# Taking every fourth weight remainder from an accumulating DMA in a two-layer trunk (GLA and spatial gating)

## The chip, the cores and the metric

The kernel runs on one core of a Trainium2 chip. The metric is the time of one execution in microseconds of device time; lower is better. The kernel before takes 775.23 us (median of two runs, 775.1 and 775.36).

## What is computed

One sequence of 256 tokens with 2048 channels goes through two layers. Layer 0 is a gated linear attention in chunks of 64 tokens, layer 1 a spatial gating with a 128 x 128 position matrix per channel group. Both begin with an RMS norm and a wide input projection, and end with an output projection and a second RMS norm. All arrays are float32.

```python
def reference(x, norm_pre, norm_post, gla_w_in, ..., sgu_w_out):
    for i in range(DEPTH):                       # DEPTH = 2
        h = rmsnorm(x, norm_pre[i])
        if i % N_MIXERS == 0:
            y = gla_mixer(h, ...)                # proj = h @ w_in; ... ; return o @ w_out
        else:
            y = sgu_mixer(h, ...)                # proj = h @ w_in; ... ; return (u * vs * silu(g)) @ w_out
        x = x + rmsnorm(y, norm_post[i])
    return x
```

Nearly all the work is in the four products with the weight matrices: 2048 x 6160 and 2048 x 2048 in layer 0, 2048 x 6144 and 2048 x 2048 in layer 1.

## The kernel before

**Tiles and steps.** The columns of the four weight matrices are cut into 33 groups, almost all of 512 columns (the three groups for the keys have 352, 344 and 344). A group's 16 K tiles of 128 rows are taken two at a time (KC = 2), so a group has 8 steps, and the program 264, numbered from 0 across all groups. Both tiles of 128 tokens (t = 0 and t = 1) use a step's weights, one after the other.

**Two parts of each number.** A product is made from float32r parts. A weight is split into `whi`, its rounded value, and `wlo`, the remainder; activations are split in the same way. Three matmuls per K tile and tile of tokens stand for one exact product (lines 178 to 180): xh·whi, xl·whi, xh·wlo. A step is thus 2 K tiles x 2 tiles of tokens x 3 = 12 matmuls.

**How a step's weights come.** `load` has SP issue a DMA of 128 x 1024 floats (512 KB) into a buffer `raw`, of which there are four (RAWS). `split` has ACT cast `raw` to `whi` (line 110), and DVE subtract `whi` from `raw` into `wlo` (line 111). At 8 steps near the start, around the layer boundary and at the end POOL subtracts in DVE's place (START, POOL). Of `whi` and `wlo` there are six buffers each (SPLITS). So the cast of step j cannot begin before the matmuls of step j - 6 are through, and the load of step j cannot begin before the split of step j - 4 has read its `raw`.

**The order.** Engines take their instructions in the order in which the program writes them. `run` writes a step's matmuls, then one stage of whatever follows earlier groups (evacuations, norms, transposes, attention), then `fetch` for the steps up to four ahead (AHEAD). Hence on ACT the cast of step 8g + 11 stands behind the evacuation of tile 0 of group g, which itself waits for the last matmul of step 8g + 7 with that tile. Around the boundary between the layers (step 136) the tiles of tokens take turns of five steps (LAG).

**Other work on POOL.** POOL carries few instructions: powers for the norms (line 224), two products per tile of tokens in the groups for u (line 703), products for the boundary (lines 605, 640), some memsets, and the 8 subtractions. It issues no DMA.

Of the kernel before, what the change touches and what calls it, by code (L numbers as in the profile page):

```python
# [9 lines left out]
F32R = mybir.dt.float32r  # L10
BF16 = mybir.dt.bfloat16
AF = mybir.ActivationFunctionType
ALU = mybir.AluOpType
PSUM = bass.MemoryType.PSUM

P = 128
# [6 lines left out]
KC = 2  # L23
LAG = 5
# [5 lines left out]
SLOTS = 24  # L30
RAWS = 4
SPLITS = 6


@with_exitstack
def trunk(
# [18 lines left out]
    nc = tc.nc  # L55
# [9 lines left out]
    of = out[0]  # L65
# [6 lines left out]
    wraw = ctx.enter_context(tc.tile_pool(name="wraw", bufs=RAWS))  # L72
    wsp = ctx.enter_context(tc.tile_pool(name="wsp", bufs=SPLITS))
    gains = ctx.enter_context(tc.tile_pool(name="gains", bufs=3))
# [12 lines left out]
    def w512(name, dtype=F32):  # L87
        return work.tile([P, 512], dtype, name=name, tag="w512")

# [1 line left out]
    def load(parts, c, fine):  # L91
        w = sum(n for _, _, n in parts)
        raw = wraw.tile([P, KC, w], F32, name="raw", tag="raw")
        at = 0
        for src, c0, n in parts:
            rows = src[c * KC * P : (c + 1) * KC * P, c0 : c0 + n].rearrange("(a p) n -> p a n", p=P)
            for ks in pieces(fine):
                nc.sync.dma_start(raw[:, ks, at : at + n], rows[:, ks, :])
            at += n
        return raw  # L100

    def pieces(fine):
        return [slice(k, k + 1) for k in range(KC)] if fine else [slice(0, KC)]

    def split(raw, eng, fine):
        shape = [P, KC, raw.shape[2]]
        hi = wsp.tile(shape, F32R, name="whi", tag="whi")
        lo = wsp.tile(shape, F32R, name="wlo", tag="wlo")
        for ks in pieces(fine):
            nc.scalar.copy(hi[:, ks], raw[:, ks])  # L110
            eng.tensor_tensor(lo[:, ks], raw[:, ks], hi[:, ks].bitcast(F32), op=ALU.subtract)  # L111
        return hi, lo

    NS = KT // KC

    class Stream:
        """Projections, column group by column group, in steps of KC K tiles; both tiles of
        tokens use a step's weights. What follows a group's products is a generator, whose
        stages come one by one between the parts that follow; a stage may ask for more parts
        before the next. Around a boundary (a group whose operand is the end of all groups  # L120
        before it) the tiles of tokens take turns of LAG steps, so that each one's products
        cover what the other waits for."""

        def __init__(self, groups, boundaries, mid):
            self.mid = mid
# [19 lines left out]
        def fetch(self, i):  # L145
            if i < len(self.steps) and i not in self.split:
                self.load(i)
                eng = nc.gpsimd if i in self.pool_lo else nc.vector
                self.split[i] = split(self.raw[i], eng, i == 0)

        def start(self, gen):
            if gen is not None:
# [35 lines left out]
        def run(self):  # L188
            freed, at = 0, 0
            for i, t in self.order:  # L190
# [4 lines left out]
                at = max(at, i)  # L195
                for j in range(at + 1, min(at + (AHEAD if at >= NS else 2), freed + SPLITS - 1) + 1):
                    self.fetch(j)
# [1 line left out]
                self.advance()  # L199

    def split_T(dst, t, c, tp):
        """Four transposed blocks, from PSUM into the two parts of a product's operand."""
        ah, al = dst
        sl = slice(t * P, (t + 1) * P)
        nc.scalar.copy(ah[c][:, :, sl], tp)  # L205
        nc.vector.tensor_tensor(al[c][:, :, sl], tp, ah[c][:, :, sl].bitcast(F32), op=ALU.subtract)  # L206
# [7 lines left out]
    def new_T(name):  # L214
        return (
            [slot(S4, F32R, f"{name}h{c}") for c in range(4)],
            [slot(S4, F32R, f"{name}l{c}") for c in range(4)],
        )
# [18 lines left out]
        return rstd(s1, D, name)  # L237

    def bcast(vecs, cs):
        """Column groups of vectors, on every partition."""  # L240
        g = gains.tile([P, 2, 512], F32, name="gb", tag="gb")
        for i, (v, c) in enumerate(zip(vecs, cs)):
            nc.sync.dma_start(
                g[:, i, :], v[c * 512 : (c + 1) * 512].unsqueeze(0).to_broadcast([P, 512])
            )
        return g

# [1 line left out]
    xs = [const.tile([P, D], F32, name=f"x{t}", tag=f"x{t}") for t in range(NT)]  # L249
    vec = const.tile([16, P], F32, name="vec")  # L250
    nc.scalar.dma_start(vec, norm_pre[0].rearrange("(a p) -> a p", p=P))
# [6 lines left out]
    make_identity(nc, ident)  # L258
    mhalf = const.tile([P, 1], F32, name="mhalf")
    nc.gpsimd.memset(mhalf, -0.5)  # L260
    # suffix sums within a chunk: U[t', t] = 1/tau where t' > t and both lie in one chunk;
    # the last two columns give the chunks' sums
    U = const.tile([P, P + 2], F32, name="U")
    nc.gpsimd.memset(U, 0.0)
    for c in range(2):
        r = slice(c * C, (c + 1) * C)
# [7 lines left out]
    gpre0 = const.tile([P, KT], F32, name="gpre0")  # L274
    bsp = const.tile([P, GROUPS], F32, name="bsp")

# [1 line left out]
    hT = new_T("hT")  # L278

    def make_hT(t, c):  # L280
        tp = transpose4(xs[t][:, c * 512 : (c + 1) * 512])
        tmp = w512("ttmp").rearrange("p (a b) -> p a b", b=P)
        gain = gpre0[:, c * 4 : c * 4 + 4].unsqueeze(2).to_broadcast([P, 4, P])
        nc.vector.tensor_tensor(tmp, tp, gain, op=ALU.mult)
        split_T(hT, t, c, tmp)
# [3 lines left out]
    groups = []  # L289

    q, k, la, ek, kd, k2, qT = ([None] * 2 for _ in range(7))
# [14 lines left out]
    for i in range(2):  # L306
        groups.append(dict(parts=[(W, q0 + i * 512, 512)], lhs=lambda: hT, done=q_done(i)))

    # the gate's weights and bias, each part at its own partitions, against the parts of the
    # low-rank activations: one pass gives all four products  # L310
    wg = [None]

    def pre_gate():
# [179 lines left out]
    for i, (c0, n) in enumerate(kcols):  # L493
        parts = [(W, k0 + c0, n)] + ([(W, l0, RANK)] if i == 0 else [])
        groups.append(dict(parts=parts, lhs=lambda: hT, done=k_done(i)))

    on = [None] * HEADS
# [58 lines left out]
    for h in range(HEADS):  # L556
        groups.append(dict(parts=[(W, g0 + h * DV, DV)], lhs=lambda: hT, done=g_done(h)))

# [1 line left out]
    def out_groups(key, w_out, gain, name, end, extra=None):  # L560
        yg = [None] * 4
        ss = [small(f"{name}ss{t}", 4) for t in range(NT)]
# [30 lines left out]

    r1 = [None] * NT

    # the second layer's operand is x1 * gain = x * gain + rstd * (y * post gain * gain)
    yp, xp = [None] * 4, [None] * 4

    def extra0(t, c, ps):
# [45 lines left out]
    groups += gs  # L645
    layer1 = len(groups)

# [1 line left out]
    W2 = sgu_w_in[0]  # L649
    vg = [None] * 4  # L650
    bst = [small(f"bst{t}", 4 * 6).rearrange("p (c s) -> p c s", s=6) for t in range(NT)]
# [42 lines left out]
    def u_done(c):  # L694
        def f(t, ps):
            if t == 0:
                u[c] = slot([P, NT, 512], F32, f"u{c}")
            nc.scalar.activation(u[c][:, t, :], ps, AF.Gelu_apprx_tanh, scale=r1[t])
            a = vg[c][:, t, :]
            mu, rv = st["ln", t]  # L700
            nc.vector.tensor_scalar(a, a, mu, rv, op0=ALU.subtract, op1=ALU.mult)  # L701
            for i, op in enumerate((ALU.mult, ALU.add)):
                nc.gpsimd.tensor_tensor(a, a, st["lng"][:, i, :], op=op)  # L703
        return f

    for c in range(4):
        groups.append(
            dict(
                parts=[(W2, c * 512, 512)], lhs=lambda: st["h2"], done=u_done(c),
# [48 lines left out]

    groups += out_groups("tT", sgu_w_out[0], norm_post[1], "y1", end1)

# [1 line left out]
    mid = {(0, 0): lambda: make_hT(1, 0), (1, 0): lambda: make_hT(0, 1)}  # L762
    for c in range(1, 4):
        mid[2 * c - 1, 1] = lambda c=c: make_hT(1, c)
# [2 lines left out]
    s = Stream(groups, [layer1, len(groups)], mid)  # L767
# [50 lines left out]
```

## Time and profile before

| | before |
|---|---|
| time, median of two runs | 775.23 us |
| span of the profiled execution | 772.0 us |
| PE busy | 755.7 us (98%) |
| DVE busy | 452.9 us (59%) |
| ACT busy | 353.7 us (46%) |
| POOL busy | 87.6 us (11%) |
| DMA engines, share of 16 engines' span in SP's queue | 59.5% |
| read from device memory | 143.55 MB |

The profiled execution's span is 3.2 us below the median time of the runs. PE's busy time counts pipelined matmuls, so it says that PE had matmuls to run nearly always, and not how fast it ran them.

### The profile page before, as it was taken

To read this page: it belongs to the slowest core of one execution; us is meant where nothing else is said; L and a number is where in the kernel's file an instruction comes from. 1 tells how busy PE (TensorE), PEld (TensorE's weight loads), DVE (VectorE), ACT (ScalarE), POOL (GpSimd) and SP (SyncE) were. 2 spreads that over 40 slices of the span, in tenths; PEclk is the share of its full clock that TensorE was granted. 3 is DMA by queue.
4 is the path that set the end of the run, shared out by engine and by line. 5 is a ranking of instruction groups with operands and counts; after the bars stand their busy time and mean duration, and the time that the engine had idled before them with its cause. 6 is when DMAs were issued, how large, how long until landed. Compare 5 with 4: busy or idle time off the path is not lost.

```text
span 772.0 us, 9465 instructions
## 1 busy us (share of the span) xinstructions
PE 755.7 (98%) x3560; PEld 633.4 (82%) x3560; DVE 452.9 (59%) x521; ACT 353.7 (46%) x473; POOL 87.6 (11%) x81
## 2 busy tenths in 40 slices
PE   8999999999999999999989999999999999999995
PEld 6889998888888888888867888888888888888884
DVE  4666764645465545766588564555556565565443
ACT  4654753534354434444446454444335445344430
POOL 3210010000000001403041000132232000000000
PEclk9999999999999999999999999999999999999998
DMA  9576583465755567664724855666766455656633
GB/s 302 162 209 186 159 259 110 136 218 165 216 166 168 169 196 232 215 219 167 264 88 137 272 190 192 196 208 215 227 217 203 152 166 169 195 182 234 203 104 110
DMA packets 81318, 146.28 MB, mean 189 GB/s; under 512 B 7196, under 2 KB 14900, under 8 KB 81272
## 3 DMA queue, kind: packets, MB, share of 16 engines
q1 hardware_dynamic: 81240, 145.66, 59.5%
q8 instruction: 28, 0.46, 0.2%
q14 instruction: 18, 0.15, 0.1%
q10 hardware_dynamic: 32, 0.01, 0.0%
HBM read 143.55 MB, written 2.10 MB: 189 GB/s over the span
## 4 chain that ended last, share of the span: by engine, by line
PE 94%; DVE 2%; issue 1%; DMA 1%; ACT 0%; SPq 0%; POOLq 0%; POOL 0%; DVEq 0%; ACTq 0%
PE acc L180 30%; PE acc L178 30%; PE acc L179 30%; PE tp L211 2%; PE op L519 1%; DVE hp L614 1%; DMA raw<-in_gla_w_in_dram 1%; PE sc L440 1%; PE sp L371 0%; PE sc L433 0%; DVE h2l L206 0%; DVE wlo L111 0%; DVE x L752 0%; DVE x L590 0%; PE sc L446 0%
## 5 line engine op out<-in xcount | busy, mean ns | idle before, releaser
L111 DVE TENSOR_TENSOR wlo<-raw,whi 128x1024 fp32r<-128x1024 f32 (+2 forms) x257 | 316.6, 1254 | 119.6 <-ACT whi L110 119.2
L110 ACT CAST whi<-raw 128x1024 fp32r<-128x1024 f32 (+3 forms) x265 | 264.7, 1021 | 141.7 <-PE acc L179 57.5
L178 PE MATMUL acc<-whi,hTh 128*128 128x512 f32 (+2 forms) x416 | 158.7, 382 | 1.4 <-ACT hTh L205 1.4
L179 PE MATMUL acc<-whi,hTl 128*128 128x512 f32 (+2 forms) x416 | 155.9, 375 | 0.2 <-DVE hTl L206 0.2
L180 PE MATMUL acc<-wlo,hTh 128*128 128x512 f32 (+2 forms) x416 | 156.0, 375 | 0.0
L178 PE MATMUL acc<-whi,h2h 128*128 128x512 f32 x384 | 151.5, 394 | 0.0
L179 PE MATMUL acc<-whi,h2l 128*128 128x512 f32 x384 | 150.0, 391 | 0.0
L180 PE MATMUL acc<-wlo,h2h 128*128 128x512 f32 x384 | 149.8, 390 | 0.0
L178 PEld LDWEIGHTS acc<-whi,hTh 128*128 128x128 f32 x416 | 78.5, 189 | 13.3 <-ACT hTh L205 1.7
L180 PEld LDWEIGHTS acc<-wlo,hTh 128*128 128x128 f32 x416 | 78.4, 189 | 12.9
L179 PEld LDWEIGHTS acc<-whi,hTl 128*128 128x128 f32 x416 | 78.6, 189 | 12.7 <-DVE hTl L206 0.6
L180 PEld LDWEIGHTS acc<-wlo,h2h 128*128 128x128 f32 x384 | 72.4, 188 | 15.3
L178 PEld LDWEIGHTS acc<-whi,h2h 128*128 128x128 f32 x384 | 72.4, 189 | 14.4
L179 PEld LDWEIGHTS acc<-whi,h2l 128*128 128x128 f32 x384 | 72.4, 189 | 14.3
L178 PE MATMUL acc<-whi,ogTh 128*128 128x512 f32 x128 | 50.2, 392 | 0.0
L178 PE MATMUL acc<-whi,tTh 128*128 128x512 f32 x128 | 50.0, 391 | 0.0
L179 PE MATMUL acc<-whi,tTl 128*128 128x512 f32 x128 | 49.8, 389 | 0.0
L180 PE MATMUL acc<-wlo,ogTh 128*128 128x512 f32 x128 | 49.8, 389 | 0.0
L180 PE MATMUL acc<-wlo,tTh 128*128 128x512 f32 x128 | 49.8, 389 | 0.0
L179 PE MATMUL acc<-whi,ogTl 128*128 128x512 f32 x128 | 49.8, 389 | 0.0
L703 POOL TENSOR_TENSOR vg<-vg,gb 128x512 f32<-128x512 f32 x16 | 27.8, 1735 | 61.4 <-DVE vg L701 41.1
L229 ACT ACTIVATE sq<-acc 128x512 bf16<-128x512 f32 x16 | 9.5, 596 | 50.3 <-PE acc L180 50.3
(155 smaller groups left out, 586.9 us busy)
## 6 DMA issues: line engine op xcount, KB each, us to landing
raw<-in_sgu_w_in_dram SPq DMA_DIRECT2D x96, 512.0 KB, 4.8
raw<-in_gla_w_in_dram SPq DMA_DIRECT2D x79, 512.0 KB, 4.6
raw<-in_gla_w_out_dram SPq DMA_DIRECT2D x32, 512.0 KB, 5.7
raw<-in_sgu_w_out_dram SPq DMA_DIRECT2D x32, 512.0 KB, 4.8
raw<-in_gla_w_in_dram SPq DMA_DIRECT2D x16, 344.0 KB, 3.7
raw<-in_gla_w_in_dram SPq DMA_DIRECT2D x8, 336.0 KB, 3.6
x<-in_x_dram SPq DMA_DIRECT2D x8, 256.0 KB, 7.4
gb<-in_norm_post_dram SPq DMA_DIRECT2D x8, 256.0 KB, 6.2
```

Of the source, the lines that this page charges most:

```text
L110: nc.scalar.copy(hi[:, ks], raw[:, ks])
L111: eng.tensor_tensor(lo[:, ks], raw[:, ks], hi[:, ks].bitcast(F32), op=ALU.subtract)
L178: nc.tensor.matmul(pt, xh, wh[:, k, :], start=kt == 0, stop=False)
L179: nc.tensor.matmul(pt, xl, wh[:, k, :], start=False, stop=False)
L180: nc.tensor.matmul(pt, xh, wl[:, k, :], start=False, stop=kt == KT - 1)
L211: nc.tensor.transpose(tp[:, k, :], src[:, k * P : (k + 1) * P], ident)
L229: nc.scalar.activation(sq[:, : src.shape[1]], src, AF.Square, accum_out=dst)
L440: nc.tensor.matmul(sc[:, o + C : o + P], k2[c][:, i, o : o + P], qT[c][:, i, o + C : o + P], start=jl == 0, stop=jl == JH - 1,)
L519: nc.tensor.matmul(op, a, b, start=i == 0, stop=i == len(ops) - 1)
L614: nc.vector.scalar_tensor_tensor(hp[c], yp[c][:, t, :], r, xp[c][:, t, :], op0=ALU.mult, op1=ALU.add)
L703: nc.gpsimd.tensor_tensor(a, a, st["lng"][:, i, :], op=op)
```

## The change

In the steps whose number is 3 modulo 4, from step 8 on and in groups with one weight part, `split` gives way to a new function `added`. There ACT writes `wlo` as minus the rounded `raw` (an activation with scale -1), then casts `raw` to `whi` as before. Then POOL issues two DMAs, one for each K tile, that read the same weights from device memory again and add them onto `wlo`. DVE (or POOL) subtracts nothing in these steps. The group of keys with two parts is left as it was, so 62 of the 264 steps change, with 124 DMAs: 58 steps of 512 columns and 4 of 344. The other lines of the diff drop comments; the changed kernel's line numbers are 19 higher behind the new code.

```diff
+ADDED = 4
...
+    def added(raw, src):
+
+        shape = [P, KC, raw.shape[2]]
+        hi = wsp.tile(shape, F32R, name="whi", tag="whi")
+        lo = wsp.tile(shape, F32R, name="wlo", tag="wlo")
+        nc.scalar.activation(lo, raw, AF.Copy, scale=-1.0)
+        nc.scalar.copy(hi, raw)
+        (w, c0, n), c = src
+        for k in range(KC):
+            r = (c * KC + k) * P
+            nc.gpsimd.dma_start(lo[:, k, :], w[r : r + P, c0 : c0 + n], accum_op=ALU.add)
+        return hi, lo
...
         def fetch(self, i):
             if i < len(self.steps) and i not in self.split:
                 self.load(i)
-                eng = nc.gpsimd if i in self.pool_lo else nc.vector
-                self.split[i] = split(self.raw[i], eng, i == 0)
+                g, c = self.steps[i]
+                parts = self.groups[g]["parts"]
+                if len(parts) == 1 and i % ADDED == ADDED - 1 and i >= NS:
+                    self.split[i] = added(self.raw[i], (parts[0], c))
+                else:
+                    eng = nc.gpsimd if i in self.pool_lo else nc.vector
+                    self.split[i] = split(self.raw[i], eng, i == 0)
```

On ACT, the place shown is the end of a group for u (`u` is the evacuation of a tile of tokens, `whi` the cast of a step's weights). Before:

```order
L698 ACTIVATE u_4267<-acc,r_3530 128x512
L110 CAST whi<-raw 128x1024
L698 ACTIVATE u_4267<-acc,r_3597 128x512
L110 CAST whi<-raw 128x1024 x7
L698 ACTIVATE u_4425<-acc,r_3530 128x512
```

The same place on ACT in the changed kernel:

```order
L717 ACTIVATE u_4347<-acc,r_3592 128x512
L111 ACTIVATE wlo<-raw 128x1024
L112 CAST whi<-raw 128x1024
L717 ACTIVATE u_4347<-acc,r_3661 128x512
L124 CAST whi<-raw 128x1024 x3
L111 ACTIVATE wlo<-raw 128x1024
L112 CAST whi<-raw 128x1024
L124 CAST whi<-raw 128x1024 x3
L717 ACTIVATE u_4509<-acc,r_3592 128x512
```

Of the eight steps between two evacuations of tile 0, two have one more ACT instruction, which stands ahead of their cast; one of the two steps is the one right behind the evacuation of tile 0.

On POOL, the place is the boundary between the layers (`y0r` is the norm's power of a tile of tokens, `xp` a product for the next layer's operand). Before:

```order
L224 TENSOR_TENSOR y0r_3305<-y0r_ms,mhalf 128x1
L605 TENSOR_TENSOR xp_3308<-x_87,gb 128x512
L111 TENSOR_TENSOR wlo<-raw,whi 128x1024 x2
L224 TENSOR_TENSOR y0r_3403<-y0r_ms,mhalf 128x1
L605 TENSOR_TENSOR xp_3308<-x_88,gb 128x512
L111 TENSOR_TENSOR wlo<-raw,whi 128x1024
L224 TENSOR_TENSOR r_3530<-r_ms,mhalf 128x1
```

The same place on POOL in the changed kernel:

```order
L116 DMA wlo<-in_gla_w_out_dram 128x512 x2
L243 TENSOR_TENSOR y0r_3365<-y0r_ms,mhalf 128x1
L624 TENSOR_TENSOR xp_3368<-x_87,gb 128x512
L125 TENSOR_TENSOR wlo<-raw,whi 128x1024
L116 DMA wlo<-in_sgu_w_in_dram 128x512 x2
L243 TENSOR_TENSOR y0r_3465<-y0r_ms,mhalf 128x1
L624 TENSOR_TENSOR xp_3368<-x_88,gb 128x512
L125 TENSOR_TENSOR wlo<-raw,whi 128x1024
L243 TENSOR_TENSOR r_3592<-r_ms,mhalf 128x1
L116 DMA wlo<-in_sgu_w_in_dram 128x512 x2
```

The second of POOL's two subtractions between the first `xp` and the second `y0r` (step 139) has become two DMA issues; elsewhere issues stand between POOL's own instructions.

## Rows read from the trace of the kernel before

**Rows 1.** The page: busy us, share of the span, instructions.
```profile
PE 755.7 (98%) x3560; PEld 633.4 (82%) x3560; DVE 452.9 (59%) x521; ACT 353.7 (46%) x473; POOL 87.6 (11%) x81
```
**Rows 2.** Waits on PE: who waited for whom, us, times, longest.
```profile
PE tp L211 <- DVE hp L614: 4.7, 3, 2.6
```
**Rows 3.** Groups by line: busy, mean ns; idle before, releaser.
```profile
L111 DVE TENSOR_TENSOR wlo<-raw,whi 128x1024 fp32r<-128x1024 f32 (+2 forms) x257 | 316.6, 1254 | 119.6 <-ACT whi L110 119.2
L110 ACT CAST whi<-raw 128x1024 fp32r<-128x1024 f32 (+3 forms) x265 | 264.7, 1021 | 141.7 <-PE acc L179 57.5 <-DMA raw<-in_gla_w_out_dram 19.9 <-DMA raw<-in_sgu_w_in_dram 18.2
L111 POOL TENSOR_TENSOR wlo<-raw,whi 128x1024 fp32r<-128x1024 f32 (+1 forms) x8 | 18.8, 2356 | 16.9 <-ACT whi L110 16.9
```
**Rows 4.** Timeline, ACT and PE, step 179: start us, us, instruction.
```profile
513.24 0.69 ACT L698 ACTIVATE u<-acc,r 128x512 f32<-128x512 f32 x1 [5.97 <-PE acc L180]
513.83 1.04 ACT L110 CAST whi<-raw 128x1024 fp32r<-128x1024 f32 x1
...
522.56 0.39 PE L178 MATMUL acc<-whi,h2h 128*128 128x512 f32 x1
523.01 0.39 PE L180 MATMUL acc<-wlo,h2h 128*128 128x512 f32 x1
```
**Rows 5.** Timeline, ACT and PE, step 183.
```profile
519.88 1.05 ACT L110 CAST whi<-raw 128x1024 fp32r<-128x1024 f32 x1 [1.60 <-PE acc L179]
...
533.44 0.39 PE L178 MATMUL acc<-whi,h2h 128*128 128x512 f32 x1
```
**Rows 6.** Timeline, ACT and PE, steps 10 and 11, then step 15.
```profile
37.89 1.98 ACT L110 CAST whi<-raw 128x1024 fp32r<-128x1024 f32 x2
...
43.44 0.39 PE L178 MATMUL acc<-whi,hTh 128*128 128x512 f32 x1
...
48.51 1.05 ACT L110 CAST whi<-raw 128x1024 fp32r<-128x1024 f32 x1 [0.30 <-DMA raw<-in_gla_w_in_dram]
```
**Rows 7.** Timeline, ACT and PE, steps 143 and 144 (casts), 143 (matmul).
```profile
416.44 1.99 ACT L110 CAST whi<-raw 128x1024 fp32r<-128x1024 f32 x2
...
423.26 0.39 PE L178 MATMUL acc<-whi,h2h 128*128 128x512 f32 x1
```
**Rows 8.** DMA: the queue's packets, MB, share; issues by line, KB, us to landing.
```profile
q1 hardware_dynamic: 81240, 145.66, 59.5%
...
raw<-in_sgu_w_in_dram SPq DMA_DIRECT2D x96, 512.0 KB, 4.8
...
raw<-in_gla_w_in_dram SPq DMA_DIRECT2D x16, 344.0 KB, 3.7
...
out_dram<-x SPq DMA_DIRECT2D x6, 256.0 KB, 2.5
```
**Rows 9.** Timeline of SP: the issue of one DMA.
```profile
506.25 0.46 SPq L243 DMA_DIRECT2D gb<-in_sgu_ln_gain_dram  x1
```
**Rows 10.** Timeline, POOL, the products of line 703 in one group.
```profile
509.06 2.65 POOL L703 TENSOR_TENSOR vg<-vg,gb 128x512 f32<-128x512 f32 x2 [11.82 <-DVE vg L701]
516.66 4.44 POOL L703 TENSOR_TENSOR vg<-vg,gb 128x512 f32<-128x512 f32 x2 [4.95 <-DVE vg L701]
```
**Rows 11.** Timeline, POOL, DVE, ACT and PE at the boundary between the layers.
```profile
393.27 2.47 POOL L111 TENSOR_TENSOR wlo<-raw,whi 128x1024 fp32r<-128x1024 f32 x1 [0.31 <-ACT whi L110]
393.43 3.40 DVE L111 TENSOR_TENSOR wlo<-raw,whi 128x1024 fp32r<-128x1024 f32 x1
...
394.32 0.59 ACT L205 CAST h2h<-tp 128x512 fp32r<-128x512 f32 x1 [1.12 <-PE tp L211]
...
397.35 0.74 DVE L614 SCALAR_TENSOR_TENSOR hp<-yp,y0r,xp 128x512 f32<-128x512 f32 x1
...
398.23 1.08 PE L211 MATMUL tp<-ident,hp 128*128 128x128 f32 x4 [2.57 <-DVE hp L614]
...
399.97 0.63 PE L180 MATMUL acc<-wlo,h2h 128*128 128x512 f32 x1
400.39 0.63 PE L178 MATMUL acc<-whi,h2h 128*128 128x512 f32 x1
```

## Prediction

> **What bounds the kernel now.** I read the page's busy times first, then PE's waits, then the groups by line, then the timeline around single steps.
>
> PE is busy for 755.7 of 772.0 us, DVE for 452.9, ACT for 353.7 and POOL for 87.6 [rows 1]. So the reader should ask whether PE runs short of work. The waits say hardly ever: the largest entry on PE is 4.7 us in three waits for `hp`, at the boundary between the layers [rows 2]. The time is therefore the matmuls' own cadence. Two matmuls lie 0.45 us apart from 522.56 to 523.01 [rows 4], 0.226 us each; the 0.39 us in the row is a pipelined length. A step of 12 matmuls takes 2.72 us, and 264 steps some 715 us (the narrow key groups a little less).
>
> None of these matmuls goes away. DVE's subtractions take 1.25 us of each 2.72 us step and ACT's casts 1.02 [rows 3], so neither engine is short either. What the change can do is make `wlo` late. The quantity to read is thus the **lead**: from the start of a step's cast to its first matmul. I paired the n-th cast with the n-th step for all steps. In the 62 changed steps there are four kinds:
> - The step behind an evacuation. The cast of step 179 starts at 513.83, right after the evacuation that waited for PE, and PE reaches the step at 522.56: a lead of 8.73 us [rows 4]. Twelve of the 62 have exactly this lead and ten more lie between 9.1 and 9.9.
> - The other changed step of a group, whose cast waits only for its buffers: from 519.88 to 533.44, 13.6 us [rows 5]. Most of the rest have 10.7 to 15.4.
> - The first changed steps, while ACT and the loads are still catching up. Step 11 has the shortest lead of all: its cast, the second of two that end at 39.87, starts about 38.83, and PE comes at 43.44, 4.6 us [rows 6]. Steps 15, 31 and 35 have 5.8, 6.4 and 5.8.
> - Step 143 behind the boundary: 416.44 to 423.26, 6.8 us [rows 7]; steps 147 and 135 have 7.4 and 7.7, and the three left 7.9 to 8.3.
>
> **The change, part by part.**
>
> *DVE's subtractions.* 62 at 1.25 us, 78 us of DVE, go. DVE isn't waited for except at the boundary, so this is worth nothing by itself.
>
> *One POOL subtraction, of step 139.* It ran from 393.27 for 2.47 us, and beside it DVE's subtraction took 3.40 us in place of 1.25 [rows 3, 11]. DVE's next `hp` came at 397.35 and PE, which had waited 2.57 us for it, began at 398.23 [rows 11]. If DVE is not slowed there, `hp` comes about 1.8 us earlier, and the matmuls behind the wait, which stand 0.42 us apart (399.97 to 400.39) [rows 11], less often run at that pace. I take 2 us as the gain. The two ACT operations of step 139 end about when `h2h` is due at 394.32 [rows 11], so ACT should not take it back.
>
> *ACT's extra operation.* 62 of about 1.05 us (the cast of the same tile, rows 4), 65 us on an engine that is busy for 46%. Each delays what stands behind it on ACT by 1 us against leads of 5 us and more: nothing.
>
> *The accumulating DMAs.* They start when ACT's `wlo` is done, 1.05 us after the old start of the cast. PE needs the first half of `wlo` for the step's third matmul, 0.45 us in, and the second half for its sixth, 1.13 us in. So the second DMA may land up to lead - 1.05 + 1.13, about lead + 0.1, after `wlo`'s first write. Call the time that it does take L.
>
> No accumulating DMA and no issue on POOL is in the trace. For the **issue**, SP's of 0.46 us [rows 9] bounds it below, and POOL's pass over a whole tile, 2.36 us [rows 3], above; I take the middle, 1.4. For the **landing**, 256 KB that are written take 2.5 us [rows 8], the lower bound. An addition has to bring two operands, 512 KB for 256 KB, and a load of 512 KB lands in 4.8 us under this kernel's own traffic [rows 8]; I take that. For the **second DMA behind the first**, the queue moved 145.66 MB in 59.5% of 772 us [rows 8], 3.15 us per MB of all engines' time, so 512 KB add 1.65 us. Then L = 1.4 + 4.8 + 1.65 = 7.9 us; at the lower bound 0.5 + 2.5 + 0.8 = 3.8. For the upper bound I take additions four times as dear as plain bytes: 1.4 + 4.8 + 3 x 1.65 for the first and 4 x 0.82 behind it, 14 us.
>
> The Trainium skill's page "DMA: Bandwidth & Descriptors" (section "Anatomy of one DMA — SWDGE (gpsimd) path") fits a DMA issued from GpSimd as 2.0 us plus the bytes over 436 GB/s, an estimated 2.6 us for 256 KB. By it everything but step 11 would be hidden and the sum would be a gain of 2 us. This trace's loads are slower than that fit (4.8 against 3.2 us for 512 KB), so I keep to the rows.
>
> With L = 7.9 the shortfalls are: step 11, 7.9 - 4.7 = 3.2 us; step 15 nothing, since its cast waits for a load, not for PE [rows 6], and PE has just fallen 3.2 us behind; step 143, 1.0; steps 147 and 135, 0.4 and 0.1; steps 31 and 35 with 344 columns (L = 2 x 1.4 + 3.7 = 6.5 from the row of 344 KB [rows 8]), 0.7 together. Sum 5.4 us.
>
> *The DMA engines.* The 31.8 MB read again are 22% of what the queue moved, so 13 points of share as plain bytes, 26 as two operands: 59.5 becomes about 86% [rows 8]. Loads get slower. They have room: four `raw` buffers give 4 x 2.72 = 10.9 us, of which load and split (4.8 + 2.3) take 7.1 [rows 3, 8].
>
> *POOL's own work behind the issues.* In the groups for u the products of tile 0 run at 509.06, well before step 179's issue, and those of tile 1 at 516.66 [rows 10]; they move back by the issues and are not needed by PE soon. Nothing.
>
> **Sum:** 772.0 - 2 + 5.4 = 775.4 us for the profiled execution; the runs' median lies 3.2 us above it, so 779 us.
>
> **Rivals.**
>
> *The DMAs are cheap.* If L is 6 us or less, only steps 11 and 15 or so are short, by 1.5 us in all: 772 - 2 + 1.5, so 775 us on the runs' scale. For it: 256 KB written in 2.5 us. Against: the operand that must be read back.
>
> *Issuing on POOL is dear, beside a busy DVE.* POOL's pairs in line 703 take 2.65 us alone and 4.44 us beside DVE's subtractions, 1.68 times as long [rows 10]. An issue of 1.4 x 1.68 = 2.35 us makes L = 2 x 2.35 + 4.8 = 9.5 us. Then all steps with a lead of 8.73 fall short by 0.7 us, and over the 62 leads the shortfalls add up to 33 us: 772 - 2 + 33, so **806 us**, slower than before. It decides from L = 8.8 on, where the dozen equal leads begin to fail: at 8.5 the shortfalls are 15 us, at 9.0 they are 22, at 10 they are 47. The margin of my forecast, 0.9 us of issue or landing, is thin.
>
> The Trainium skill's page "SBUF — State Buffer" (section "SBUF: two separate sides") states such a mechanism: while DVE runs an operation in a two-port mode, GpSimd can't write descriptors, and a DMA of about 620 ns takes about 3100 ns. The trace has no such DMA to show it on; that POOL's own work slows beside DVE is all that the rows show. The page also says that DVE's `tensor_tensor`, most of its work here, has no such mode, which speaks for less.
>
> *Additions cost the DMA engines far more than bytes.* At four times, share becomes 59.5 + 52, over 100%, which alone makes the span about 1.12 x 772 = 865 us; and by the leads, the shortfalls add up to 160 us at L = 13 and 211 at 14. After waits like the one at 398.23 the matmuls ran at half their pace for a few [rows 11], which adds. About 900 us, 865 to 980. Nothing in the rows excludes it.
>
> **How the numbers follow.** My forecast (L from 6 to 8.7 us, 775 to 788) gets 0.36, the cheap case 0.18, the dear issue 0.26, dear additions 0.20. The likeliest is 779 us. A measurement of this kernel can tell 2%, 15.5 us. Faster by more would need a PE that runs faster or waits that aren't there (4.7 us in all at the boundary): 0.01. The first two cases are within 2%, and a little of the third's lower edge: 0.54. Slower: 0.45. The range from 770 to 880 leaves out most of the far half of the last case and little else; the likeliest case's own range is 775 to 788.
>
> **What would show it.** Each DMA group of `wlo` landing 5 to 7 us after its issue; POOL's issues at 1 to 2 us; PE waiting for a `wlo` at step 11 for about 3 us and hardly at all behind evacuations; the boundary's wait for `hp` down from 2.57 us; the DMA share near 85%. Wrong would be: a wait of PE on `wlo` in every group (then L is above 8.8, and POOL's issue or the landing says which), a share near 100% with casts waiting for loads, or `hp` no earlier.

## The result and the profile after

The changed kernel takes 793.41 us (median of two runs, 792.31 and 794.51) against 775.23: 1.0235 times as long, 95% interval 1.0201 to 1.0269. It is slower, by a little more than 2%. The profiled execution's span is 790.6 us against 772.0, so the trace has 18.6 us to be explained.

The page's busy line (engine, busy us, share of the span, instructions), to be read beside [rows 1]:

```profile
PE 762.9 (96%) x3560; PEld 632.7 (80%) x3560; DVE 386.5 (49%) x460; ACT 410.2 (52%) x535; POOL 186.6 (24%) x204
```

DVE has lost 66 us, ACT has gained 57, POOL 99, and PE has as many instructions as before. What PE now waits for (who waited for whom, us in all, times, longest), against [rows 2]:

```profile
PE acc L199 <- DMA wlo<-in_gla_w_in_dram: 5.6, 5, 2.1
PE acc L199 <- DMA wlo<-in_gla_w_out_dram: 5.3, 3, 3.7
PE acc L199 <- DMA wlo<-in_sgu_w_in_dram: 3.7, 4, 1.5
...
PE tp L230 <- DVE hp L633: 1.0, 2, 0.6
```

Twelve waits for a `wlo` that a DMA writes, 14.6 us; the wait for `hp` has fallen from 4.7 to 1.0 us. The groups by line (busy us, mean ns of one, idle before), against [rows 3]:

```profile
L125 DVE TENSOR_TENSOR wlo<-raw,whi 128x1024 fp32r<-128x1024 f32 (+2 forms) x196 | 247.5, 1281 | 175.6 <-ACT whi L124 174.9
...
L116 POOL DMA_DIRECT2D wlo<-in_gla_w_in_dram x44 | 39.1, 1050 | 187.9 <-ACT wlo L111 182.4
...
L111 ACT ACTIVATE wlo<-raw 128x1024 fp32r<-128x1024 f32 (+1 forms) x62 | 64.4, 1039 | 36.5 <-DMA raw<-in_sgu_w_in_dram 21.6
...
L116 POOL DMA_DIRECT2D wlo<-in_sgu_w_in_dram x48 | 42.4, 1037 | 129.0 <-ACT wlo L111 122.0
```

An issue takes POOL 1.04 us, and in all but three of the 62 pairs the second begins 0.54 to 0.61 us after the first. The queues (packets, MB, share of 16 engines) and the landings (KB each, median us from issue to landing), against [rows 8]:

```profile
q1 hardware_dynamic: 81240, 145.66, 55.3%
q0 software_dynamic: 17856, 31.83, 25.5%
...
raw<-in_sgu_w_in_dram SPq DMA_DIRECT2D x96, 512.0 KB, 5.8
...
raw<-in_gla_w_out_dram SPq DMA_DIRECT2D x32, 512.0 KB, 7.0
...
wlo<-in_sgu_w_in_dram POOLq DMA_DIRECT2D x48, 256.0 KB, 6.8
wlo<-in_gla_w_in_dram POOLq DMA_DIRECT2D x36, 256.0 KB, 7.0
```

The reader should see that 256 KB added onto SBUF take about as long to land as 512 KB loaded, or longer (7.1 us against 7.0 in the output projection of layer 0, 6.8 to 7.0 against 5.6 to 5.9 elsewhere), and that the loads have become 1.0 to 1.3 us slower.

**Where the 18.6 us lie.** I set the last matmul of each step and tile of tokens beside the same one of before, and noted each place where the difference moves by 0.25 us or more. From step 40 to 126, and from 151 to 262, there is no such place, though four fifths of the accumulating DMAs are there. The losses are at nine steps (all in us). The lead after runs from the start of ACT's write of `wlo` to the moment at which PE reaches the step; L is, as in the prediction, the time from the end of that write to the landing of the second DMA:

| step | lead before | lead after | L | L - (lead after + 0.1) | predicted | lost there in the trace |
|---|---|---|---|---|---|---|
| 11 | 4.6 | 4.5 | 7.7 | 3.1 | 3.2 | 3.13 |
| 15 | 5.8 | 5.9 | 9.1 | 3.1 | 0 | 3.22 |
| 31 | 6.4 | 6.4 | 6.8 | 0.3 | 0.7 with 35 | 0.42 |
| 35 | 5.8 | 6.3 | 6.7 | 0.3 | | 0.33 |
| 127 | 8.0 | 4.5 | 9.6 | 5.0 | 0 | 5.10 |
| 135 | 7.7 | 7.9 | 9.5 | 1.5 | 0.1 | 1.52 |
| 139 | 12.9 | 9.3 | 11.1 | 1.7 | 0 | 1.66 |
| 143 | 6.8 | 6.8 | 8.9 | 2.0 | 1.0 | 2.03 |
| 147 | 7.4 | 7.4 | 8.7 | 1.2 | 0.4 | 1.19 |

The last column adds up to 18.6 us. Behind the waits at 11 and 127 another 3.35 us go, 1.36 at step 11 and 1.37 + 0.62 at 127 and 128. The boundary gives back 3.59 at step 136 and 1.34 behind it. Moves at steps 0 to 10 (-1.26, 0.40, 0.27 and 0.54), ahead of the first step that an accumulating DMA feeds, cancel out. The rest, about 1.5 us, is the last step's 0.26 and moves under 0.25.

A step that is hidden, 179, on ACT, POOL and PE (start us, us, instruction), against [rows 4]:

```profile
531.91 1.05 ACT L111 ACTIVATE wlo<-raw 128x1024 fp32r<-128x1024 f32 x1
...
533.25 1.78 POOL L116 DMA_DIRECT2D wlo<-in_sgu_w_in_dram  x2 [3.00 <-ACT wlo L111]
```

ACT's write ends at 532.96, POOL issues at 533.25, the DMAs land at 538.41 and 540.62, and PE needs the second half at 541.77: L is 7.7 us, and 1.2 us are to spare. Between step 51 and 123, and from 155 on, the steps behind an evacuation have L of 6.6 to 9.0 us and 0.2 to 3.2 us to spare.

**The two places that the prediction had at nothing.** The chain of work that ended last, from step 11 to step 15 of the changed kernel (start us, us, what):

```profile
40.11 1.95 POOL wlo L116 x2
42.06 0.98 POOL wgr L334
...
43.05 4.26 DMA wgr<-in_gla_w_gate_dram
...
47.86 4.97 DMA raw<-in_gla_w_in_dram
...
52.93 1.07 ACT wlo L111
...
54.83 8.30 DMA wlo<-in_gla_w_in_dram
```

Step 11's issues wait on POOL for ACT, and the memset of the gate's buffer stands behind them. SP waits for that memset with the gate's loads, and the loads of steps 14 and 15 stand behind those on SP (first at 47.37, before at 42.77). So step 15 is written at 52.93 where its cast was at 48.51 [rows 6]. PE was 4.5 us late by then too, so the lead stayed 5.9 us, and L was 9.1.

The chain ahead of step 127:

```profile
362.40 1.74 DVE wlo L125
364.14 0.26 SPq L262
...
366.44 7.14 DMA raw<-in_gla_w_out_dram
...
373.69 1.07 ACT wlo L111
...
375.63 8.76 DMA wlo<-in_gla_w_out_dram
384.43 0.81 PE acc L199
```

What SP waits for ahead of the loads of gains, in the kernel before and then in the changed one (us, times, longest):

```profile
SPq L243 <- DVE yp L604: 9.5, 1, 9.5
...
SPq L262 <- POOL xp L624: 10.9, 1, 10.9
```

Here the lead was not kept. PE would have come at 378.2, and the write began at 373.69. The product `xp` stands on POOL behind the issues of step 123, and SP waits for it. Four loads of gains then went ahead on SP (363.06 to 364.44), where before had two. Step 127's load was issued at 366.44, 12.2 us later than before (354.22), while PE was 8.9 us later, and took 7.1 us. So 3.5 us of the lead were gone.

**The half pace.** The windows behind the waits at steps 11 and 127 (us, busy us and instructions of PE, PEld, DVE, ACT, POOL; granted clock, DMA share, GB/s):

```profile
47.60:50.30 2.70, 2.70 (x7) 2.14 (x8) 0.00 (x0) 0.00 (x0) 0.00 (x0) 0.50 0.59 127
50.30:53.00 2.70, 2.70 (x13) 2.23 (x12) 0.37 (x1) 1.12 (x2) 0.00 (x0) 0.96 1.05 376
...
384.40:388.40 4.00, 3.97 (x9) 3.13 (x10) 1.29 (x2) 3.14 (x6) 1.21 (x3) 0.50 0.85 289
```

A granted clock of 0.50 is the lower level, 1.2 GHz: 7 matmuls in 2.70 us, and 13 in the next 2.70 us. In the trace the clock is at 0.50 from 47.2 to 50.5 us and from 381.7 to 388.4. PE had stood still before, except for three matmuls, from 44.52 to 47.55, and for 3.71 us before 382.53.

### The profile page after: what moved, and what is told of

Read it like the earlier page. It is cut to its first block, busy times and chain, and to the rows that moved or that the text cites. A ratio compares the mean times of both kernels' runs of the same rounds, so it can differ in the third digit from the quotient of the medians.

```text
span 790.6 us, 9740 instructions
## 1 busy us (share of the span) xinstructions
PE 762.9 (96%) x3560; PEld 632.7 (80%) x3560; DVE 386.5 (49%) x460; ACT 410.2 (52%) x535; POOL 186.6 (24%) x204
## 3 DMA queue, kind: packets, MB, share of 16 engines
q0 software_dynamic: 17856, 31.83, 25.5%
## 4 chain that ended last, share of the span: by engine, by line
PE 78%; DMA 11%; DVE 4%; issue 3%; ACT 3%; POOL 1%; SPq 0%; POOLq 0%; DVEq 0%; ACTq 0%
PE acc L199 25%; PE acc L198 24%; PE acc L197 24%; DMA wlo<-in_gla_w_in_dram 3%; DMA wlo<-in_gla_w_out_dram 2%; PE tp L230 2%; DMA wlo<-in_sgu_w_in_dram 2%; DVE wlo L125 1%; DMA raw<-in_gla_w_in_dram 1%; ACT wlo L111 1%; PE op L538 1%; DMA raw<-in_gla_w_out_dram 1%; DVE hp L633 1%; DMA wlo<-in_sgu_w_out_dram 1%; DMA raw<-in_sgu_w_out_dram 1%
## 5 line engine op out<-in xcount | busy, mean ns | idle before, releaser
L125 DVE TENSOR_TENSOR wlo<-raw,whi 128x1024 fp32r<-128x1024 f32 (+2 forms) x196 | 247.5, 1281 | 175.6 <-ACT whi L124 174.9
L124 ACT CAST whi<-raw 128x1024 fp32r<-128x1024 f32 (+3 forms) x203 | 201.8, 1018 | 109.9 <-DMA raw<-in_gla_w_in_dram 40.6
L197 PEld LDWEIGHTS acc<-whi,hTh 128*128 128x128 f32 x416 | 78.6, 189 | 12.9 <-ACT hTh L224 1.2
L116 POOL DMA_DIRECT2D wlo<-in_gla_w_in_dram x44 | 39.1, 1050 | 187.9 <-ACT wlo L111 182.4
L197 PEld LDWEIGHTS acc<-whi,h2h 128*128 128x128 f32 x384 | 72.1, 188 | 14.1
L111 ACT ACTIVATE wlo<-raw 128x1024 fp32r<-128x1024 f32 (+1 forms) x62 | 64.4, 1039 | 36.5 <-DMA raw<-in_sgu_w_in_dram 21.6
L116 POOL DMA_DIRECT2D wlo<-in_sgu_w_in_dram x48 | 42.4, 1037 | 129.0 <-ACT wlo L111 122.0
L112 ACT CAST whi<-raw 128x1024 fp32r<-128x1024 f32 (+1 forms) x62 | 63.1, 1019 | 0.0
```

The lines of the kernel that those rows point to most:

```text
L111: nc.scalar.activation(lo, raw, AF.Copy, scale=-1.0)
L112: nc.scalar.copy(hi, raw)
L116: nc.gpsimd.dma_start(lo[:, k, :], w[r : r + P, c0 : c0 + n], accum_op=ALU.add)
L197: nc.tensor.matmul(pt, xh, wh[:, k, :], start=kt == 0, stop=False)
```

## The experiments

Ratios are to the kernel before, run beside each kernel on the same chip. The theories are: **A**, a few steps with a short lead lose what L exceeds it by; **B**, the traffic of all the accumulating DMAs costs time by itself, through slower loads; **C**, ACT's extra operation delays what stands behind it; **D**, POOL's queue makes loads late, by the two chains above. Losses at steps are read, as above, from the one profiled execution of each run, which need not be the median one.

### Long leads only

```diff
-                if len(parts) == 1 and i % ADDED == ADDED - 1 and i >= NS:
+                if len(parts) == 1 and i % ADDED == ADDED - 1 and i >= NS and i not in (11, 15, 127, 135, 143, 147):
```

> The changed kernel with six of its 62 changed steps (11, 15, 127, 135, 143, 147) split by ACT and DVE as before; 56 steps, 112 of 124 accumulating DMAs, stay. Theory A (the loss is PE waiting for wlo at the few steps whose cast has a short lead; everywhere else the DMA is hidden): the waits on wlo go from 14.6 us to under 4 us and the time falls to 771 to 777 us. Rival B (the loss is the added traffic and issue work as such, spread over the program): 90% of it stays, 789 to 792 us.

Measured: 777.48 us, ratio 1.0046 [1.0033, 1.0060]. That is 0.5 us above A's range and 11.5 below B's: six steps of 62 carry four fifths of the loss. The waits for a `wlo` from a DMA fall from 14.6 to 1.0 us with 90% of the traffic left. The trace loses 0.75 us at steps 31 and 35, 0.9 at 131 and 0.75 at 163 and 171, where L is just over the lead. The profiled execution is the fastest of the eight (774.96 us); where the median lost its 2.5 us more is in no trace.

### The same traffic, and nobody waits for it

The DMAs add onto a tile that nobody reads; DVE subtracts as before; ACT writes as much as in the changed kernel and two tiny pieces more.

```diff
+    spare = const.tile([P, KC, 512], F32R, name="spare")
...
+        for k in range(KC):
+            nc.scalar.activation(spare[:, k, 0:2], raw[:, k, 0:2], AF.Copy, scale=-1.0)
         nc.scalar.copy(hi, raw)
+        nc.vector.tensor_tensor(lo, raw, hi.bitcast(F32), op=ALU.subtract)
...
-            nc.gpsimd.dma_start(lo[:, k, :], w[r : r + P, c0 : c0 + n], accum_op=ALU.add)
+            nc.gpsimd.dma_start(spare[:, k, :n], w[r : r + P, c0 : c0 + n], accum_op=ALU.add)
```

> ACT's extra write, POOL's 124 issues and the 124 accumulating DMAs stay, but they add onto a spare tile that nobody reads, and DVE makes wlo by subtracting, as before (one buffer less of 24 for slots, to make room; the output is complete). Theory A (it is the wait for the accumulated wlo): no wait of PE on a DMA of wlo, and 770 to 777 us; the loads stay slower (5.6 us and more for 512 KB in place of 4.8). Rival B (the traffic slows the loads or the matmuls): still 786 to 795 us.

Measured: 780.99 us, ratio 1.0095 [1.0077, 1.0112]. That lies between the two ranges. So issues and traffic are not free, but their price lies at two places, 2.5 us at step 14 and 5.75 at step 127, where the two chains above end. At 127 PE waits for a subtraction of DVE:

```profile
PE acc L205 <- DVE wlo L118: 4.0, 1, 4.0
```

The loads were late (ACT waited 10.4 us for that of step 126, and step 127's came behind it), and the subtraction took 5.7 us in place of 1.25 beside POOL's products at that place. At the other steps it loses at most 0.4 us (step 19), apart from moves at step 10 and behind the boundary that the two runs without accumulating DMAs show too. So slower loads alone are nearly hidden there.

### No DMAs at all

```diff
-        for k in range(KC):
-            r = (c * KC + k) * P
-            nc.gpsimd.dma_start(lo[:, k, :], w[r : r + P, c0 : c0 + n], accum_op=ALU.add)
```

> The changed kernel without its 124 DMAs: in the 62 steps the second part stays minus the first part, so the remainder is left out there. ACT's extra operation and the missing 62 subtractions stay. Theory A: what is left is the boundary's gain, 767 to 772 us. Rival C (ACT's extra operation ahead of casts and evacuations costs PE time): above 775 us.

Measured: 771.08 us, ratio 0.9966 [0.9954, 0.9978]. With ACT's extra operation in it, this is the most that taking 62 subtractions off DVE and POOL gives, and the trace has all of it at the boundary: 3.58 us at step 136, 0.6 behind it, 1.05 lost again at once, 3.2 net. So theory C is out: a kernel with ACT's extra operation is no slower than before.

### The kernel before, with step 139's subtraction on DVE

```diff
-POOL = (1, 3, 5)
+POOL = (1, 5)
```

> The kernel before with one edit: at the boundary DVE in place of POOL makes the remainder of the fourth step behind it (step 139; POOL = (1, 5)). If the gain that the changed kernel shows at the boundary (4.9 us against the steps around it) comes from taking that subtraction off POOL, where it slowed DVE's subtraction from 1.2 to 3.4 us: 770 to 773 us. If it comes from DVE having fewer subtractions there, or from the other changed steps: 774 to 777 us.

Measured: 772.39 us, ratio 0.9980 [0.9971, 0.9989]. Without one DMA the same 3.58 us come at step 136 (2.4 net). PE's longest wait for `hp` falls from 2.6 us [rows 2] to 0.8:

```profile
PE tp L211 <- DVE hp L614: 2.2, 4, 0.8
```

So the boundary's gain comes from taking this subtraction off POOL, as the prediction had it, and it comes even where DVE has to do it instead. This version is faster than both kernels, by 0.2% against before.

### POOL's other work moved ahead of the issues

The memset moves to an earlier group, and both tiles' products `xp` are written at tile 0's stage.

```diff
+            if i == 0 and t == 0:
+                wgr_early[0] = slot([P, DK], F32, "wgr")
+                nc.gpsimd.memset(wgr_early[0], 0.0)
...
+            for tt in range(NT):
+                nc.gpsimd.tensor_tensor(
+                    xp[c][:, tt, :], xs[tt][:, c * 512 : (c + 1) * 512], gp, op=ALU.mult
+                )
```

> The changed kernel with all 62 accumulating steps, but with two pieces of POOL's own work written ahead of the DMA issues behind which they stood: the memset of wgr (ahead of step 11's) and the products xp of the second tile of tokens (beside those of the first, so ahead of the issue of the steps behind an evacuation). Theory D (an issue on POOL waits for ACT, POOL's own work waits behind the issue, SP's small loads wait for that work, and the loads of the weights wait behind them on SP): the loss at steps 14 and 15 (3 us) and at step 127 (about 6.5 us) goes, ratio to before 1.008 to 1.014. Rival B (the added traffic makes those loads late): the ratio stays at 1.020 or more.

Measured: 792.26 us, ratio 1.0248 [1.0234, 1.0262]: no better, and in B's range. Theory D was half right. At the start the chain is gone: step 15 is written at 50.51 in place of 52.93 and loses 1.90 us in place of 3.22. Ahead of step 127 SP now waits 8.3 us for DVE's `yp`, and the loads, issued at 360.56 in place of 364.97, take 8.0 us. Step 127 loses 5.6 us in place of 7.1, and step 135, which is met earlier, 6.4 in place of 1.5.

### The same, with long leads except at 15 and 127

```diff
-POOL = (1, 3, 5)
+POOL = (1, 5)
...
-                if len(parts) == 1 and i % ADDED == ADDED - 1 and i >= NS:
+                if len(parts) == 1 and i % ADDED == ADDED - 1 and i >= NS and i not in (11, 31, 35, 135, 139, 143, 147):
```

> The same, and the steps with short leads (11, 31, 35, 135, 139, 143, 147) split by ACT and DVE; POOL = (1, 5), so that step 139 is DVE's. 55 steps keep their accumulating DMAs, 89% of the added traffic. Theory A with D (only short leads and POOL's queue cost anything): the ratio of the kernel without any DMA, 0.995 to 0.999, a shade faster than before. Rival B (traffic): 1.004 or more.

Measured: 785.21 us, ratio 1.0163 [1.0144, 1.0182], far from the range of A with D, and in B's. Two steps alone cost 3.1 us (15) and 8.0 us (127 with its half-pace matmuls). The boundary's gain did not come in this kernel: PE waited 3.5 us for `hp`. In the trace POOL's two products `xp`, now written together (400.09, 2.98 us), push its remaining subtraction there back to 403.03, and DVE's subtraction beside it takes 3.42 us, as in [rows 11]; `hp` comes at 407.49.

### Plain copies

```diff
-            nc.gpsimd.dma_start(lo[:, k, :], w[r : r + P, c0 : c0 + n], accum_op=ALU.add)
+            nc.gpsimd.dma_start(lo[:, k, :], w[r : r + P, c0 : c0 + n])
```

> The changed kernel with the 124 DMAs as plain copies, the same bytes without the addition; the second part is then the whole weight, so the product counts it twice. If the addition is what makes a DMA long (two operands): landing 4 to 5.5 us in place of 6.8 to 7.1, their share of the DMA engines 13% in place of 25.5%, and PE's waits on wlo well under half. If issuing on POOL is what makes it long: landing within 0.7 us of before and the share near 13% all the same.

Measured once: 785.86 us, 1.016 times the kernel before beside it (773.54), where the changed kernel is at 1.0235. Queue and landings:

```profile
q0 software_dynamic: 17856, 31.83, 15.9%
...
wlo<-in_sgu_w_in_dram POOLq DMA_DIRECT2D x48, 256.0 KB, 5.0
wlo<-in_gla_w_in_dram POOLq DMA_DIRECT2D x36, 256.0 KB, 5.3
```

The addition costs 1.6 times the engines' time of a copy of the same packets (25.5% of 790.6 us against 15.9% of 784.2) and, by group, 0.9 to 1.8 us of landing. PE's waits for a `wlo` from a DMA fall from 14.6 to 9.5 us only, not to under half. Step 11 loses 0.64 us in place of 3.13, but steps 15 and 127 still lose 5.4 and 6.1, the half-pace matmuls behind them included: there the load is late (leads of 2.7 and 3.4 us) whatever the DMA does.

### One DMA for a step

```diff
-        for k in range(KC):
-            r = (c * KC + k) * P
-            nc.gpsimd.dma_start(lo[:, k, :], w[r : r + P, c0 : c0 + n], accum_op=ALU.add)
+        rows = w[c * KC * P : (c + 1) * KC * P, c0 : c0 + n].rearrange("(a p) n -> p a n", p=P)
+        nc.gpsimd.dma_start(lo, rows, accum_op=ALU.add)
```

> The changed kernel with one accumulating DMA of 512 KB for a step in place of two of 256 KB; nothing else. If two issues and two completions cost (0.7 us between the issues, one more completion): the last half lands 0.5 to 1 us earlier, but the first half no earlier than the second, so PE, which needs the first half 0.7 us before the second, waits longer at short leads: ratio 1.020 to 1.030. If the halves were slowed by sharing the engines with loads: ratio under 1.018.

Measured: 806.61 us, ratio 1.0432 [1.0400, 1.0465], above what either side had expected. The 512 KB land in 8.1 to 8.9 us, and PE needs them all by the third matmul and no longer by the sixth. Now steps behind an evacuation begin to fail too (83, 115, 171, 195, 203, 243, 251, 259, 0.3 to 1.1 us each). So the margin of the hidden steps is as thin as it was predicted, about 1 us.

### Without steps 15 and 127

> The changed kernel, but steps 15 and 127 are split as before; 60 steps accumulate. PE lost 3.2 us at step 15 and 7.1 us at step 127, where the cast came late and the second DMA then took 9 to 10 us after ACT's write. Theory A (a short lead at a few steps, each step's loss its own): those 10 us come back, step 11 keeps its 3 to 4.5 us, steps 135 to 147 keep 4 to 8 us; ratio to the kernel before 1.006 to 1.013. Theory B (the traffic of all accumulating DMAs makes the next loads late, whatever these two steps do): 97% of the traffic stays, PE waits for the cast or DVE's remainder at the same two places for 5 us or more; ratio 1.015 or above.

The edit is the condition of the first experiment with `(15, 127)`. Measured: 785.67 us, ratio 1.0162 [1.0147, 1.0177], worse than A's 1.006 to 1.013 and in B's range. But nothing is lost at the two places where B had it. The two steps had cost 10 us, and only 7 came back in the trace (span 783.8). PE reached step 131 earlier and lost 2.5 us there, where it had lost nothing, and at step 135 3.3 and 1.7 more in half-pace matmuls behind it. The chain that ends at step 135 shows why:

```profile
363.14 8.14 DMA raw<-in_gla_w_out_dram
...
373.03 5.91 DMA raw<-in_gla_w_out_dram
...
381.07 6.71 DMA raw<-in_gla_w_out_dram
...
389.81 8.12 DMA wlo<-in_gla_w_out_dram
397.93 0.04 issue
397.97 0.50 PE acc L199
```

For 35 us loads, and the splits that free their buffers, set the pace: after the burst at 363 the four `raw` buffers catch up only slowly. So a step's lead there depends on how late PE already is, and the losses of neighbouring steps replace each other.

### Short leads only

> The changed kernel, but only the ten steps 11, 15, 31, 35, 127, 131, 135, 139, 143 and 147 accumulate, 20 DMAs in place of 124; the other 52 changed steps are split as before. Theory A (short leads at these places): nearly the whole loss stays, PE waits 10 to 14 us in all for a part written by DMA; ratio 1.018 to 1.024. Theory B (traffic): with 16% of it left the loss goes with it; ratio below 1.008.

The condition ends in `i in (11, 15, 31, 35, 127, 131, 135, 139, 143, 147)`: ten steps and 16% of the traffic. Measured: 790.54 us, ratio 1.0222 [1.0194, 1.0250]: nearly all of the loss. For that much of it this decides for A against B. What PE waits for:

```profile
PE acc L199 <- DMA wlo<-in_gla_w_in_dram: 4.5, 3, 2.1
PE acc L199 <- DMA wlo<-in_gla_w_out_dram: 3.5, 4, 1.3
PE acc L199 <- DMA wlo<-in_sgu_w_in_dram: 2.3, 3, 1.0
```

Step 123 issues nothing here. PE comes to step 127 as late as in the changed kernel (378.39 against 378.20 us), but the step's load is issued at 363.34 in place of 366.44, so the step keeps its lead (8.3 us); L is 9.9 and it loses 1.57 us. So of the 5.10 us in the changed kernel about 1.5 were L, and about 3.5 the late load. (With the issues of step 123 and the steps before their traffic is gone too, so the run doesn't separate POOL's queue from it.) L of 9.2 to 9.9 at steps 15, 127 and 131 with hardly another accumulating DMA about also says that these DMAs aren't each other's hindrance there. Beside them lie the loads: within 4 us of those DMAs two were issued at steps 127 and 131, and six at step 15. That these are the cause is likely, but no run moved them away.

### No short leads, and POOL = (1, 5)

> The changed kernel without accumulation in the nine steps 11, 15, 31, 35, 127, 135, 139, 143 and 147 (53 steps are left with 106 DMAs), and with POOL = (1, 5), so that step 139's subtraction is DVE's and not POOL's. Theory A: PE waits for no part written by DMA for more than 1 us in all, the boundary gives its 3 to 4 us; ratio 0.996 to 1.002, like the kernel before with POOL = (1, 5) at 0.998, and no better, since PE sets the pace. Theory B (traffic makes loads late at the start and ahead of step 127): 2 to 6 us lost there; ratio 1.003 to 1.008.

Measured: 776.93 us, ratio 1.0042 [1.0029, 1.0055], in B's range and not in A's. But the trace puts 1.9 us on one more step, 131 (L 9.3), whose lead I had taken for long enough; against the kernel before with POOL = (1, 5) it loses nothing else above 0.25 us. Here too the profiled execution (774.81 us) is faster than the median. The last run took that step out too.

### 52 hidden steps, and POOL = (1, 5)

> As the run without the nine short steps and with POOL = (1, 5), but step 131, where PE still lost 1.9 us waiting for a part written by DMA, is split as before too; 52 steps with 104 DMAs are left, 84% of the traffic. Theory A (what is hidden costs nothing, what is late costs its shortfall): PE waits for no part written by DMA for more than 0.3 us, the ratio to the kernel before is that of the kernel before with POOL = (1, 5) alone, 0.998, within 0.002; 52 subtractions fewer on DVE buy nothing. Theory B (traffic itself costs): 1.002 or above.

Measured: 774.06 us, ratio 1.0010 [0.9999, 1.0020]. No wait for a DMA's `wlo` is left in PE's waits:

```profile
PE tp L230 <- DVE hp L633: 2.2, 4, 0.8
PE acc L197 <- ACT hTh L224: 1.4, 1, 1.4
PE warm L795 <- POOL ident masks.py:199: 1.4, 1, 1.4
PE acc L199 <- DVE wlo L125: 1.0, 1, 1.0
PE acc L198 <- DVE hTl L225: 0.2, 1, 0.2
```

With 84% of the traffic the kernel is as fast as before, to 0.2% at most, and 52 subtractions fewer on DVE bring nothing. It lies 0.001 above the range that A gave, and 0.003 above the kernel before with POOL = (1, 5). The profiled executions of these two differ by 1.6 us, of which 1.5 lie at steps 136 and 137: there the granted clock was at 0.50 from 408.1 to 411.4 us in this one, and at 1.00 in the other. What made it fall in one of them, and whether a small price of the traffic is in the medians, stays open.

## Why the prediction was right or wrong

The forecast was 779 us, no measurable change; the kernel takes 793, just over the 2%. The range held it, but 793 lies above the likeliest case's own 775 to 788, and the range reached there for the sake of two dear cases, neither of which came: that it held is luck in part. Most of the loss came by the mechanism of the forecast, short leads, at a size that was off.

**Right.** PE's matmuls set the time, and what the change cost came through a late `wlo`; leads and L are the right pair of numbers. With the L and the lead of the changed kernel, the prediction's rule (may land up to lead + 0.1) gives the loss of each of the nine steps within 0.2 us. L = 7.9 us holds for the hidden steps (7.7 at step 179), if by other terms: POOL starts 0.29 us after ACT instead of taking 1.4, the first half lands 5.2 us after its issue instead of 4.8, and the second 2.2 us behind it instead of 1.65. (The upper bound for the issue, 2.36 us for a whole tile, was a mean of six whole tiles, 2.64 us, and two halves; it didn't matter.) ACT's extra operation cost nothing that the run without DMAs could show. The boundary's gain of 2 us was 3.2 and 2.4 net in the two runs without accumulating DMAs. The share of 86% was 81%.

**Wrong: one L for all steps.** This is the term that was mis-sized. Six of the nine steps that fail have L of 8.7 to 11.1 us; so have most of the second changed steps of a group (8.4 to 10.5 us), whose long leads hide it. The landing row that I took, 4.8 us, was that of one group of loads. The same view of before has this row for the output projection of layer 0, where steps 127 and 135 are, and in the changed kernel loads were slower by another 1.0 to 1.3 us:

```profile
raw<-in_gla_w_out_dram SPq DMA_DIRECT2D x32, 512.0 KB, 5.7
```

With each step's own L and the leads of before, the rule gives 3.0 + 3.2 + 0.3 + 0.8 + 1.5 + 1.7 + 2.0 + 1.2 = 13.7 us instead of 5.4.

**Wrong: "step 15 nothing".** The prediction said that its cast waits for a load and not for PE, and took it that PE's delay would lengthen the lead. The load became late by just as much, through POOL's queue and SP's (4.4 us), so the lead stayed 5.9.

**Wrong: loads "have room", and so leads stay.** 7.1 of 10.9 us is a mean over the ring. Ahead of step 127 four loads are issued within 2 us (353.74 to 355.70) behind two of gains in the trace of before, and the cast there waits for its `raw`; the prediction read neither:

```profile
359.93 1.05 ACT L110 CAST whi<-raw 128x1024 fp32r<-128x1024 f32 x1 [6.77 <-DMA raw<-in_gla_w_out_dram]
```

Step 127 lost 3.5 us of its lead. Step 139 lost 3.6 of 12.9, and not by a load: its write stands on ACT behind a cast that waits for PE at step 134, and what the boundary gives back lies between that wait and step 139. In the changed kernel:

```profile
409.38 0.59 ACT L224 CAST h2h<-tp 128x512 fp32r<-128x512 f32 x1 [0.97 <-PE tp L230]
...
409.86 1.06 ACT L111 ACTIVATE wlo<-raw 128x1024 fp32r<-128x1024 f32 x1
```

The write came 17.7 us later than the cast of before (392.14), as PE did at step 134; PE came to step 139 only 14.1 us later (419.18 against 405.06). The prediction counted the boundary's gain and this step's lead side by side and did not take the one from the other. These two steps are the other 5 us or so.

**Wrong: "POOL's own work behind the issues: nothing".** I had looked at the groups for u alone. The memset and the first `xp` stand behind issues that wait for ACT, and SP waits for both. By the run that moved them this was worth 1.3 us at step 15, and at step 127 nothing that stayed.

**Left out of the sum.** The matmuls at half the clock behind the waits, 3.35 us; the rows of the boundary had shown such a stretch [rows 11], and it was used for the boundary's gain and for a rival, but not behind the shortfalls of the sum.

**The rivals.** The cheap case (L of 6 us or less) didn't come: the changed kernel has L of 6.6 us and more at every step, and with plain copies 43 of the 62 steps are still above 6. The dear issue didn't either: issues take 0.85 to 1.25 us everywhere, and of the steps that keep a lead of 8.73 us all but one have about 1 us or more to spare (171 has 0.2). Where a slower kernel was forecast, it was by this rival and by dear additions, so "slower" came by another way. Additions do cost more than bytes, 1.6 times a copy and not four times.

## What to carry over

A part that moves to a DMA is paid for at its shortest lead and not at the mean: list the lead of every moved instance, and take the landing time of the stretch in which each one lies. Steps that start late or follow a burst of loads should keep the engine that made the part before. Behind a DMA issue that itself waits for another engine, put nothing that loads wait for. What the change gives back between a part's start and its use comes off that part's lead. And don't add up the losses of neighbouring steps on a ring that is still catching up: taking one away moves its wait to the next. Where PE sets the time, work taken off another engine is worth only what PE had waited for, here one subtraction at the boundary.

## What the runs showed of the hardware

An accumulating DMA from device memory onto SBUF, 128 x 512 floats issued by POOL, lands in a median of 6.8 to 7.1 us under this load, a plain copy in 5.0 to 6.2, and in its packets' time it costs 1.6 times a copy. One accumulating DMA of 512 KB lands in 8.1 to 8.9 us. The issue occupies POOL for 0.85 to 1.25 us, in a kernel whose DVE is busy for 49% of the time.

The granted clock was at 0.50 around the ends of the waits at steps 11 (47.2 to 50.5 us) and 127 (381.7 to 388.4), and not at step 15:

```profile
61.00:64.00 3.00, 1.76 (x7) 1.15 (x8) 0.76 (x2) 0.79 (x2) 0.00 (x0) 1.00 1.10 323
```

PE was busy for only 1.76 of these 3.00 us, and the clock stayed at 1.00. A wait's price here is thus its length and, at two of the nine steps, the half-speed matmuls behind it.
